# A delta-net kernel whose 32x32 forward substitutions move from VectorE to GpSimd

## The chip, the cores and the metric

The kernel runs on one core of one Trainium2 chip. The metric is the device time of one execution in microseconds, lower is better. Each core has TensorE (PE, matmuls, with weight loads shown apart as PEld), VectorE (DVE), ScalarE (ACT), GpSimd (POOL) and SyncE (SP, which here only issues DMAs). Every engine works through its own instruction list in order.

## The reference

Three blocks of a small model over 256 positions of width 1024: a gated delta net with a gated MLP, sliding-window attention with a gated MLP, and a block with gated linear attention, latent attention and an MLP. The change touches the first stage only, the delta net:

```python
qkv = silu(causal_dwconv(qkv, conv_w))                  # width 4
m = where(strict, einsum('bnhcd,bnhsd->bnhcs', k_beta, k) * decay, 0.0)
t_mat = triangular_solve(m + eye, eye, left_side=True, lower=True, unit_diagonal=True)
u = einsum('bnhcs,bnhse->bnhce', t_mat, v_beta)
w = einsum('bnhcs,bnhsd->bnhcd', t_mat, k_beta * exp(gc)[..., None])
```

There are 16 heads; for each, and for each stretch of the sequence, a unit lower triangular matrix has to be inverted before the values can be mixed.

## The kernel before

All weights come from HBM as 512 KB tiles of 128x1024 (`wr`, loaded by SP, line 172). Each is split into two matmul operands: ScalarE rounds it (`wh`, line 186) and VectorE takes the difference (`wl`, line 187, two inputs in SBUF). Every product is then three matmuls (lines 249 to 251). Each of `wr`, `wh` and `wl` has four buffers, and one weight tile feeds 8 blocks of 128x128, so 24 matmuls.

The delta-net stage (`gdn_body`) is written as generators. The projections (`gemm`, `gemm_nat`) run one after another in the order of `ORDER`; each fourth weight block calls `tick`, which advances every side generator by one step. The side generators are:

- `conv`, called when a bank of q, k or v is ready: one ScalarE scaling (line 647), six VectorE multiply-adds that read the bank from PSUM (`cy`, line 650), one ScalarE SiLU (line 651).
- `x_stage` makes the triangular matrices in `XA` and writes their diagonal 32x32 blocks to HBM (`s1`, line 714).
- `inv_stage` reads the 128 blocks back, one per partition (`NT`, line 749, a DMA of the GpSimd queue), sets `TI` to the identity (lines 750 and 751, GpSimd) and does the forward substitution in 31 steps of two instructions (lines 757 and 759): step j multiplies a column of `NT` by row j of `TI` into `fst`, (31-j)(j+1) elements a partition, and adds `fst` onto the rows below. Then VectorE transposes each block into `TP` (line 764), SP writes `TI` and `TP` to HBM (lines 765 and 766) and reads them back into `XA` and `T64` in 14 small DMAs (lines 770 and 773).
- `a_stage` makes the attention blocks (`kq`, lines 729 to 733) and `chain`, four times, uses the inverses: `y1p` (line 823), `z1p`, `y2p`, `z2p`, and on to the gated output, whose matmuls with `w_out` end the stage.

The order of the instructions in each engine's list is not that of the code: a planner sorts them when the kernel is built, by the order in the code, but takes a later instruction first when it expects the earlier one not to be ready. `NT`, `TI` and `TP` share two buffers, `fst` has one.

Of the kernel before, what the change touches and what calls it, by code (L numbers as in the profile page):

```python
# [14 lines left out]
ALU = mybir.AluOpType  # L15
# [4 lines left out]
P = 128  # L20
# [122 lines left out]
class Builder:  # L143
# [432 lines left out]
    def gdn_body(self, gp, x):  # L576
        nc, tc, sp = self.nc, self.tc, self.sp
# [166 lines left out]
        def inv_stage():  # L744
            while st["X"] < 8:
                yield
            NT = t4([P, 32, 32], "NT")
            TI = t4([P, 32, 32], "TI")
            Q[1].dma_start(NT, s1.rearrange("b c h s t -> (b c h) s t"))
            nc.gpsimd.memset(TI, 0.0)  # L750
            nc.gpsimd.memset(TI.rearrange("p a b -> p (a b)")[:, 0:1024:33], 1.0)
            for _ in range(INVW):
                yield
            for j in range(31):
                m = 31 - j
                tmp = gp.tile([P, 256], F32, tag="fst", bufs=1, name="fst")[:, : m * (j + 1)].rearrange("p (a b) -> p a b", a=m)
                nc.vector.tensor_tensor(tmp, NT[:, j, j + 1 :].unsqueeze(2).to_broadcast([P, m, j + 1]),  # L757
                                        TI[:, j, 0 : j + 1].unsqueeze(1).to_broadcast([P, m, j + 1]), ALU.mult)
                nc.vector.tensor_tensor(TI[:, j + 1 :, 0 : j + 1], TI[:, j + 1 :, 0 : j + 1], tmp, ALU.add)  # L759
                st["step"] = j + 1  # L760
                if INVS(j):
                    yield
            TP = t4([P, 32, 32], "TP")
            nc.vector.tensor_copy(TP.rearrange("p c i -> p i c"), TI)
            Q[2].dma_start(s3.rearrange("b c h s t -> (b c h) s t"), TP)
            Q[2].dma_start(s2.rearrange("b c h s t -> (b c h) s t"), TI)
            nc.gpsimd.memset(T64[0:32, :, :, 32:64], 0.0)
            for b in range(4):
                for tt in range(2):
                    Q[3].dma_start(XA[blk(b), :, 2 * tt, blk(b)], s3[b, tt].rearrange("h c i -> c h i"))  # L770
                    if b < 3:
                        c = (0, 32, 0)[b]
                        Q[3].dma_start(T64[blk(b), tt, :, c : c + 32], s2[b, tt].rearrange("h i c -> i h c"))
            for _ in range(WINV):
                yield
            st["inv"] = True
# [158 lines left out]
        gz = self.gemm_nat("w_in", x, KD, [4096, 4608, 5120, 5632], 512, evac_z)  # L935
        self.side(x_stage())
        self.side(inv_stage())
        self.side(a_stage())
        for q4 in range(4):
# [995 lines left out]
```

## Time and profile before

| | us |
|---|---|
| median of 3 runs | 1226.88 (1225.82 to 1230.05) |
| the profiled execution | 1229.75 |
| its span | 1228.0 |
| busy PE / DVE / ACT / POOL | 1192.3 / 894.4 / 689.5 / 25.1 |
| the inversion's 62 VectorE instructions, busy | 20.8 |
| first one starts / last one starts | 100.83 / 149.25 |

The profile times every instruction of one execution from the start of its span. Busy is time in which an engine worked; idle time before an instruction is shown in brackets with what ended it. The profiled execution took 1.75 us more than its span.

### The profile page before, as it was taken

What the parts mean: (1) busy time and instruction counts of PE and PEld (TensorE: products, weight loads), DVE (VectorE), ACT (ScalarE), POOL (GpSimd) and SP (SyncE); (2) the same over time, 40 slices, a digit from 0 to 9 for tenths busy, and PEclk for the clock granted to TensorE, in tenths of its full rate; (3) what the DMA queues carried; (4) which work ended last, traced back from release to release, by engine and by line L of the source; (5) the groups of instructions that cost most, each with busy time, mean ns of one, the idle gap of its engine ahead of it and who ended that gap; (6) DMA issues with size and microseconds to landing.
All of it is one profiled execution on the core that took longest, in us unless ns stands there. A gap on an engine that the chain in (4) does not pass through costs nothing.

```text
span 1228.0 us, 23416 instructions
## 1 busy us (share of the span) xinstructions
PE 1192.3 (97%) x9368; PEld 1128.1 (92%) x9368; DVE 894.4 (73%) x1677; ACT 689.5 (56%) x1174; POOL 25.1 (2%) x47
## 2 busy tenths in 40 slices
PE   7999989999699999989999999999999999999997
PEld 6989878999699999979999999989889998999996
DVE  6978966668487778887987777766665567655555
ACT  5786546456265557564755556745465545444443
POOL 2000000000000000000000000000000000000000
PEclk9999999999899999999999999999999999999999
DMA  6546474355975566543465555364245564556562
GB/s 227 169 136 222 141 192 164 111 165 152 166 236 188 189 188 203 175 139 130 162 207 189 185 181 172 101 211 145 91 148 178 188 213 150 174 187 188 180 185 83
DMA packets 68989, 209.13 MB, mean 170 GB/s; under 512 B 18197, under 2 KB 18325, under 8 KB 68624
## 3 DMA queue, kind: packets, MB, share of 16 engines
q1 hardware_dynamic: 65600, 194.77, 49.4%
q0 software_dynamic: 3280, 12.87, 4.5%
q8 instruction: 73, 1.20, 0.4%
q14 instruction: 36, 0.29, 0.1%
HBM read 199.75 MB, written 7.86 MB: 169 GB/s over the span
## 4 chain that ended last, share of the span: by engine, by line
PE 83%; DVE 7%; issue 5%; DMA 3%; ACT 2%; POOL 0%; SPq 0%; DVEq 0%; ACTq 0%; POOLq 0%
PE pb L249 19%; PE pb L251 19%; PE pb L250 19%; PE acc L249 6%; PE acc L250 6%; PE acc L251 6%; DMA wr<-wall 2%; DVE wl L187 2%; DVE cy L650 1%; DMA wzog<-wzd 1%; PE ssb L669 1%; DVE fst L757 0%; DVE TI L759 0%; PE s L1082 0%; PE kv L1541 0%
## 5 line engine op out<-in xcount | busy, mean ns | idle before, releaser
L187 DVE TENSOR_TENSOR wl<-wr,wh 128x1024 fp32r<-128x1024 f32 x362 | 441.2, 1223 | 188.7 <-ACT wh L186 188.1
L186 ACT ACTIVATE wh<-wr 128x1024 fp32r<-128x1024 f32 x362 | 381.4, 1057 | 345.4 <-issue 88.5
L251 PE MATMUL pb<-xh,wl 128*128 128x256 f32 x1224 | 347.7, 284 | 11.4 <-DVE wl L187 11.3
L249 PE MATMUL pb<-xh,wh 128*128 128x256 f32 x1224 | 351.0, 287 | 2.9 <-ACT wh L186 2.4
L250 PE MATMUL pb<-xl,wh 128*128 128x256 f32 x1224 | 346.6, 283 | 0.2 <-DVE xl L570 0.2
L251 PEld LDWEIGHTS pb<-xh,wl 128*128 128x128 f32 x1224 | 232.7, 190 | 12.8 <-DVE wl L187 12.8
L249 PEld LDWEIGHTS pb<-xh,wh 128*128 128x128 f32 x1224 | 233.0, 190 | 5.6 <-ACT wh L186 2.9
L250 PEld LDWEIGHTS pb<-xl,wh 128*128 128x128 f32 x1224 | 233.0, 190 | 0.5 <-DVE xl L570 0.4
L249 PE MATMUL pb<-fh,wh 128*128 128x256 f32 x416 | 118.8, 286 | 0.0
L251 PE MATMUL pb<-fh,wl 128*128 128x256 f32 x416 | 117.6, 283 | 0.0
L250 PE MATMUL pb<-fl,wh 128*128 128x256 f32 x416 | 117.2, 282 | 0.1
L249 PE MATMUL acc<-ah,wh 128*128 128x256 f32 x352 | 98.7, 280 | 0.0
L251 PE MATMUL acc<-ah,wl 128*128 128x256 f32 x352 | 98.6, 280 | 0.0
L250 PE MATMUL acc<-al,wh 128*128 128x256 f32 x352 | 98.6, 280 | 0.0
L250 PEld LDWEIGHTS pb<-fl,wh 128*128 128x128 f32 x416 | 78.8, 189 | 1.2 <-DVE fl L436 0.5
L249 PEld LDWEIGHTS pb<-fh,wh 128*128 128x128 f32 x416 | 78.4, 189 | 1.5 <-issue 0.4
L251 PEld LDWEIGHTS pb<-fh,wl 128*128 128x128 f32 x416 | 78.3, 188 | 0.0
L977 DVE SCALAR_TENSOR_TENSOR fy<-fpad,cols,fy 128x256 f32<-128x256 f32 x176 | 73.6, 479 | 0.0
L249 PE MATMUL pb<-wh,xh 128*128 128x512 f32 (+1 forms) x176 | 70.1, 400 | 0.0
L250 PE MATMUL pb<-wl,xh 128*128 128x512 f32 (+1 forms) x176 | 67.8, 385 | 0.5 <-DVE wl L187 0.5
L251 PE MATMUL pb<-wh,xl 128*128 128x512 f32 (+1 forms) x176 | 67.9, 386 | 0.0
L249 PEld LDWEIGHTS acc<-ah,wh 128*128 128x128 f32 x352 | 66.3, 188 | 0.0
(438 smaller groups left out, 2100.7 us busy)
## 6 DMA issues: line engine op xcount, KB each, us to landing
wr<-wall SPq DMA_DIRECT2D x362, 512.0 KB, 3.7
bd<-brow POOLq DMA_DIRECT2D x1, 3072.0 KB, 36.1
wzd<-zt POOLq DMA_DIRECT2D x8, 256.0 KB, 3.4
wzog<-wzd POOLq DMA_DIRECT2D x4, 512.0 KB, 5.7
bias<-bd POOLq DMA_DIRECT2D x4, 512.0 KB, 6.9
h<-xT SPq DMA_DIRECT2D x4, 256.0 KB, 3.7
h<-xT POOLq DMA_DIRECT2D x1, 1024.0 KB, 5.6
wrow<-wrow POOLq DMA_DIRECT2D x1, 1024.0 KB, 8.7
```

The costliest lines, as they stand in the source:

```text
L186: nc.scalar.activation(hi, r, AF.Copy)
L187: i = nc.vector.tensor_tensor(lo, r, hi.bitcast(F32), ALU.subtract)
L249: mm(out, ah, bh, start=start, stop=False, skip_group_check=skip)
L250: mm(out, ah, bl, start=False, stop=False, skip_group_check=skip)
L251: mm(out, al, bh, start=False, stop=stop, skip_group_check=skip)
L650: nc.vector.scalar_tensor_tensor(y[:, i, n:], u[:, : T - n], w(j), y[:, i, n:], ALU.mult, ALU.add)
L669: nc.tensor.matmul(ssb[:, c : c + 1], sq[:, i, tt * P : tt * P + P], self.ones[:, 0:1], start=True, stop=True)
L977: nc.vector.scalar_tensor_tensor(y[:, i], u[:, i, j : j + T], w(j), y[:, i], ALU.mult, ALU.add)
```

## The change

Both instructions of each of the 31 substitution steps are issued to GpSimd in place of VectorE. Shapes, operands, buffers and their order in the code stay as they are.

```diff
             for j in range(31):
                 m = 31 - j
                 tmp = gp.tile([P, 256], F32, tag="fst", bufs=1, name="fst")[:, : m * (j + 1)].rearrange("p (a b) -> p a b", a=m)
-                nc.vector.tensor_tensor(tmp, NT[:, j, j + 1 :].unsqueeze(2).to_broadcast([P, m, j + 1]),
+                nc.gpsimd.tensor_tensor(tmp, NT[:, j, j + 1 :].unsqueeze(2).to_broadcast([P, m, j + 1]),
                                         TI[:, j, 0 : j + 1].unsqueeze(1).to_broadcast([P, m, j + 1]), ALU.mult)
-                nc.vector.tensor_tensor(TI[:, j + 1 :, 0 : j + 1], TI[:, j + 1 :, 0 : j + 1], tmp, ALU.add)
+                nc.gpsimd.tensor_tensor(TI[:, j + 1 :, 0 : j + 1], TI[:, j + 1 :, 0 : j + 1], tmp, ALU.add)
```

## Rows read from the trace of the kernel before

**Rows 1.** Page, part 1: busy time, share of the span, instructions.

```profile
PE 1192.3 (97%) x9368; PEld 1128.1 (92%) x9368; DVE 894.4 (73%) x1677; ACT 689.5 (56%) x1174; POOL 25.1 (2%) x47
```

**Rows 2.** Windows: stretch, length, busy by engine, granted clock, DMA share, GB/s.

```profile
100.00:150.00 50.00, 48.49 (x365) 46.24 (x366) 48.01 (x129) 27.15 (x41) 1.08 (x2) 1.00 0.50 161
...
110.00:120.00 10.00, 10.00 (x87) 10.00 (x86) 10.00 (x26) 5.10 (x8) 0.00 (x0) 1.00 0.53 171
130.00:140.00 10.00, 8.49 (x70) 8.14 (x69) 9.77 (x33) 5.25 (x9) 0.00 (x0) 1.00 0.10 34
150.00:160.00 10.00, 8.32 (x41) 6.34 (x40) 9.45 (x17) 5.18 (x10) 0.00 (x0) 1.00 1.03 224
170.00:180.00 10.00, 8.27 (x103) 7.53 (x92) 7.50 (x14) 6.63 (x10) 0.00 (x0) 0.90 0.24 69
```

**Rows 3.** Groups of VectorE instructions from 100 to 150 us.

```profile
L187 DVE TENSOR_TENSOR wl<-wr,wh 128x1024 fp32r<-128x1024 f32 x13 | 15.8, 1218 | 1.2 <-ACT wh L186 1.2
L650 DVE SCALAR_TENSOR_TENSOR cy<-pb,cols,cy 128x255 f32<-128x255 f32 (+2 forms) x30 | 14.3, 475 | 0.2 <-ACT cy L647 0.2
L759 DVE TENSOR_TENSOR TI<-TI,fst 128x31 f32<-128x31 f32 (+15 forms) x31 | 10.4, 336 | 0.2
L757 DVE TENSOR_TENSOR fst<-NT,TI 128x31 f32<-128x31 f32 (+15 forms) x31 | 10.4, 334 | 0.1
```

**Rows 4.** Timeline of PE: the matmuls that waited, and the first `y1p`.

```profile
138.34 0.39 PE L251 MATMUL pb<-xh,wl 128*128 128x256 f32 x1 [1.51 <-DVE wl L187]
...
152.85 0.50 PE L250 MATMUL pb<-wl,xh 128*128 128x512 f32 x1 [0.55 <-DVE wl L187]
...
159.36 0.66 PE L789 MATMUL vtp<-ident,vt 128*128 128x128 f32 x4 [1.13 <-ACT vt L651]
...
163.10 0.24 PE L823 MATMUL y1p<-h,XA 32*32 32x32 f32 x2
...
176.77 0.39 PE L251 MATMUL pb<-xh,wl 128*128 128x256 f32 x1 [1.74 <-DVE wl L187]
```

**Rows 5.** Timeline of ScalarE: one weight rounding.

```profile
125.58 1.06 ACT L186 ACTIVATE wh<-wr 128x1024 fp32r<-128x1024 f32 x1 [1.42 <-PE pb L250]
```

**Rows 6.** Timeline of VectorE: first and last substitution, two late subtractions.

```profile
100.83 0.18 DVE L757 TENSOR_TENSOR fst<-NT,TI 128x31 f32<-128x31 f32 x1
...
137.07 1.21 DVE L187 TENSOR_TENSOR wl<-wr,wh 128x1024 fp32r<-128x1024 f32 x1
...
149.25 0.18 DVE L759 TENSOR_TENSOR TI<-TI,fst 128x31 f32<-128x31 f32 x1
...
151.59 1.21 DVE L187 TENSOR_TENSOR wl<-wr,wh 128x1024 fp32r<-128x1024 f32 x1
```

**Rows 7.** Timeline of SP: the inverse written, the next weight loads.

```profile
149.50 0.33 SPq L766 DMA_DIRECT2D s<-TI  x1
...
152.86 0.33 SPq L172 DMA_DIRECT2D wr<-wall  x1
...
161.89 72.54 SPq L172 DMA_DIRECT2D wr<-wall  x16
```

**Rows 8.** The tile `NT`: its one DMA, issue to landing.

```profile
DMA to landing us min/median/max: 5.9/5.9/5.9
```

**Rows 9.** Groups of GpSimd instructions, shapes apart: busy us, mean ns.

```profile
L750 POOL MEMSET TI<- 128x1024 f32 x1 | 1.0, 973 | 0.0
...
L594 POOL MEMSET gch<- 128x384 f32 x1 | 0.4, 422 | 0.0
...
L589 POOL CAST identb<-ident 128x128 bf16<-128x128 f32 x1 | 0.3, 299 | 5.0 <-DMA ident<-cst 5.0
L524 POOL MEMSET ones<- 128x128 f32 x1 | 0.2, 204 | 0.3 <-POOLq L1923 0.3
L751 POOL MEMSET TI<- 128x32 f32 x1 | 0.2, 162 | 0.1
...
L1923 POOL MEMSET const-float32-1.0<- 128x1 f32 x1 | 0.1, 93 | 0.0
```

**Rows 10.** Timeline of VectorE, 14 to 32 us.

```profile
20.99 4.63 DVE L187 TENSOR_TENSOR wl<-wr,wh 128x1024 fp32r<-128x1024 f32 x4
```

**Rows 11.** Timeline of GpSimd, 0 to 100 us.

```profile
20.18 0.95 POOL L767 MEMSET h<- 32x1024 f32 x1 [2.09 <-DVE xn L568]
21.08 4.90 POOL L588 CAST mask3b<-mask 128x384 bf16<-128x384 f32 x1
...
94.79 0.54 POOL L749 DMA_DIRECT2D NT<-s  x1 [17.87 <-DMA s<-XA]
```

## The prediction

> **What bounds the kernel now.** I read the page first, then the windows of the delta-net stage, then who waits inside them. TensorE is busy 1192.3 of 1228.0 us [rows 1], so what a change can win is TensorE's idle time in the stage it touches, and what it can lose is new idle time there. The substitutions run from 100.83 to 149.43 us [rows 6], 48.6 us for 62 instructions that are busy only 20.8 us [rows 3], because VectorE's list alternates them with other work: VectorE is busy 48.0 of the 50 us from 100 to 150 [rows 2]. It is the saturated helper of that stretch, TensorE the engine that sets the end.
>
> TensorE still works without a gap for most of it. Its matmuls come every 10/87 = 0.115 us [rows 2], so one weight tile (24 matmuls) lasts 2.76 us. Four gaps stand between 130 and 180 us [rows 4]: 1.51 us at 138.34 and 0.55 us at 152.85, both ended by a weight subtraction `wl`; 1.13 us at 159.36, ended by a conv's SiLU; 1.74 us at 176.77, again `wl`. The first three are VectorE's backlog. The ninth rounding after 100 us is done by ScalarE at 126.64 [rows 5], its subtraction, the ninth too, starts at 137.07 [rows 6], over 10 us late; the gap at 138.34 follows directly. The subtraction at 151.59 [rows 6] ends the second gap, and it also frees a `wr` buffer: SP issues the next weight load at 152.86 [rows 7], and the ScalarE work in front of the SiLU waits for weights. The fourth gap is less clear: the weight loads also stand behind the inverse's small DMAs, from 152.86 to 161.89 [rows 7], and that remains.
>
> **What the change takes from VectorE.** 62 instructions, 10.4 + 10.4 = 20.8 us [rows 3]. VectorE's load from 100 to 150 us falls from 48.0 to 27.2 us. The subtractions then follow their roundings, and three gaps should close: 1.51 + 0.55 + 1.13 = 3.2 us. I leave the fourth, 1.74 us, for the range. VectorE's saved 20.8 us are worth no more than that, since TensorE has nothing else to wait for.
>
> **What it puts on GpSimd.** The trace before shows no two-input instruction there, so the price is built from the nearest ones [rows 9]. A memset goes from 204 ns for 128 elements to 422 ns for 384: 0.85 ns an element that is written. The smallest takes 93 ns, so about 0.09 us is fixed. The cast of 128 elements, one read and one write, takes 299 ns: (299 - 93)/128 = 1.61 ns, hence 0.76 ns for a read. Two reads and a write: 2.37 ns. The steps have 5456 elements a partition (the sum of (31-j)(j+1) over j = 0 to 30), twice over, 10912: 25.9 us. Fixed: 62 x 0.09 = 5.6 us. Rows of `TI` are not contiguous: the memset of 32 scattered elements takes 162 ns, (162 - 93)/32 = 2.2 ns each against 0.85, so 1.3 ns for a jump; 496 row starts in each of three operands add 1.9 us. Sum 33.4 us undisturbed. Lower bound: an element at the price of the cast, 5.6 + 10912 x 0.00161 = 23.2 us. Upper bound: every element at the scattered ratio 2.2/0.85, that is 6.1 ns, 72 us. I take the middle value, since each of its parts is a row.
>
> GpSimd does not run undisturbed. The cast of 384 elements should take 0.09 + 384 x 0.00161 = 0.7 us; it took 4.90 us, from 21.08 to 25.98 [rows 11], over four subtractions back to back that took 4.63 us from 20.99 to 25.62 [rows 10], the usual 1.16 us each. So GpSimd stood still while VectorE read two SBUF operands, and VectorE lost nothing. From 100 to 150 there are 13 such subtractions [rows 3], 13 x 1.16 = 15.1 us, 30% of the time. The convolutions read their bank from PSUM and one operand from SBUF; I take them as no hindrance. The substitutions then need 33.4/0.70 = 47.9 us, and 1.1 us more for the two GpSimd DMA issues that lie in the window [rows 2]: 49.0 us. They cannot start earlier, since `NT` is issued at 94.79 [rows 11] and takes 5.9 us to land [rows 8], 100.7. They end at 149.8, against 149.4 before: a loss of 0.4 us.
>
> The Trainium skill speaks against the change and for the hindrance. "SBUF — State Buffer", section "Who interferes with whom", says that a VectorE instruction with two SBUF inputs and a GpSimd instruction that reads SBUF use one shared read interface, and that the later one waits for the whole of the earlier. By that rule, the cast's row agrees for GpSimd's side (4.90 us for an estimated 0.7); that a subtraction is held by GpSimd no row here shows. "GPSIMD Engine Reference", section "3. Performance versus the Vector engine", has 4497 ns for a two-input add of 2048 elements; as an estimate from that page 2.2 ns an element, and the sum would be 31.5 us in place of 33.4, the end 146.9 in place of 149.8.
>
> **What waits for the end of the substitutions.** VectorE's transpose copy, SP's write of `TI` and the 14 small DMAs behind it, then `y1p` on TensorE, 163.10 - 149.43 = 13.7 us after the last step [rows 4, 6]. TensorE did not idle before the first `y1p`, so there is little slack: I count each microsecond of delay as one of TensorE time. Behind the copy on VectorE stand the subtractions and convolutions, behind the write on SP the weight loads, behind `y1p` on TensorE the projections. Where the planner puts them matters: it does pull instructions ahead, as the memset of line 767, which the code has behind the substitutions, ran at 20.18 [rows 11]. I assume that it places the copy about where the data are.
>
> GpSimd has no other work to delay but DMA issues (1.1 us in this window [rows 2]); they are queued behind at most one step of 0.7 us. That costs nothing while a spare `zt` buffer covers it, and 0.7 us otherwise.
>
> **Sum.** -3.2 + 0.4 = -2.8 us. The profiled execution, 1229.75 us, becomes 1226.95; it stood 2.87 us above the median of the runs, so the runs become 1226.88 - 2.8 = 1224.1 us. A measurement of this kernel tells about 0.3%, 3.7 us, from no change, so this is a gain near the limit.
>
> **Rivals.**
>
> GpSimd is slower than the rows say, the substitutions end late and TensorE waits at `y1p`: slower. The point from which it decides is close. The gain is eaten when they take 48.6 + 3.2 = 51.8 us; the run is slower by over 3.7 us from 55.5 us, an element price of ((55.5 - 1.1) x 0.70 - 7.5)/10912 = 2.8 ns in place of 2.37. At half as much again, 3.6 ns, it is 46.8/0.70 + 1.1 = 68 us, 19.4 us late, 1226.9 + 19.4 - 3.2 = 1243. For it: the scattered memset's 2.2 ns, and that no row shows two reads; against it: the middle price is put together from undisturbed rows. Chance 0.25.
>
> The planner believes in a faster GpSimd than there is and puts the transpose copy early into VectorE's list. Had it counted the undisturbed 33.4 us, the copy would stand at 134, when GpSimd has 0.30 x 33.4 = 10 us left; VectorE then waits 10 us with the subtractions behind the copy. TensorE has up to three weight tiles in hand, 8.3 us, and fewer if the lead is two, 5.5 us. It idles 1.7 to 4.5 us, and catching up can cost as much again: 1225.5 to 1232, middle 1229. For it: the 20.18 memset shows that it pulls ahead; against it: before, no list was held at the copy. Chance 0.12.
>
> The change does nothing in the end: the subtractions wait for GpSimd as often as GpSimd for them, 13 times up to 0.7 us, or the gaps come from the late weight loads and stay: 1226.9. For it: SP's 9 us of small DMAs [rows 7]. Chance 0.08.
>
> More is won: the fourth gap closes too, and with it the granted clock of 0.90 from 170 to 180 [rows 2], a mean between its levels of 2.4 and 1.2 GHz, is whole again, about 1 us: 1226.9 - 3.2 - 1.7 - 1.0 = 1221. For it: a VectorE at 54% lets weight tiles be prepared deeper, which would bridge SP's 9 us. Chance 0.10.
>
> **How the numbers follow.** The forecast has 0.45, with its own range 1221 to 1227 (GpSimd's end 3 us earlier or later, the fourth gap in or out). About half of it, 0.22, is faster by over 0.3%, 0.23 within. Add 0.10 faster; 0.25 slower; of the planner's case 0.07 slower and 0.05 within; 0.08 within. Faster 0.32, same 0.36, slower 0.32. The range reaches down to 1219 and up to 1239, so that the worst half of the slow GpSimd and a little below are left out.
>
> **What would show it.** Right: VectorE busy about 27 of the 50 us from 100 to 150; subtractions within 2 us of their roundings; the gaps at 138 and 153 us gone; the largest GpSimd steps at 0.7 us alone and near 1.8 us when a subtraction falls on them; the last step near 150 us, `y1p` near 163 without idle time. Wrong: a step of over 0.8 us with no subtraction beside it; an idle VectorE in front of the copy of line 764 or TensorE in front of line 823; convolutions that hold GpSimd as well, which would take 30 x 0.4 us more.

## The result, and the profile after

The changed kernel takes 1250.34 us (median of 4 runs, 1249.14 to 1251.74), the kernel before beside it 1228.36 (1225.82 to 1230.05): ratio 1.0177 [1.0159, 1.0196], about 22 us slower, where 2.8 us less were forecast. The profiled execution took 1249.57 us, its span is 1247.7.

The page of the kernel after, part 1 (busy time) and two rows of part 2 (tenths in 40 slices of 31 us):

```profile
PE 1193.0 (96%) x9368; PEld 1129.3 (91%) x9368; DVE 883.4 (71%) x1615; ACT 689.3 (55%) x1174; POOL 63.6 (5%) x109
...
PE   7999399999889999998999999999999999999997
...
PEclk9999699999989999999999999999999999999999
```

TensorE does the same work in the same busy time [rows 1]. The fifth slice, 125 to 156 us, is at 3 tenths with TensorE's granted clock at 6 tenths: the loss has one place. Windows of the kernel after around it (columns as in [rows 2]), and the whole stage:

```profile
120.00:130.00 10.00, 10.00 (x85) 9.95 (x84) 6.02 (x9) 5.24 (x8) 9.14 (x12) 1.00 0.51 160
130.00:140.00 10.00, 3.98 (x34) 3.78 (x32) 0.00 (x0) 0.00 (x0) 8.88 (x15) 0.85 0.00 0
140.00:150.00 10.00, 0.00 (x0) 0.00 (x0) 1.02 (x2) 0.00 (x0) 7.56 (x18) 0.50 0.00 0
150.00:160.00 10.00, 5.84 (x36) 5.79 (x37) 9.75 (x20) 6.45 (x12) 0.00 (x0) 0.63 0.87 238
...
100.00:260.00 160.00, 136.00 (x1309) 126.87 (x1309) 95.37 (x215) 77.76 (x161) 44.39 (x73) 0.91 0.47 147
```

The same stretch of the kernel before:

```profile
100.00:260.00 160.00, 154.24 (x1476) 144.07 (x1477) 121.13 (x314) 86.51 (x184) 5.92 (x11) 0.99 0.51 160
```

From 130 to 149 us VectorE, ScalarE and the DMA engines stand still, from 134 us TensorE too, and GpSimd alone works. TensorE's idle time in the stage grew from 160 - 154.24 = 5.8 to 160 - 136.00 = 24.0 us, 18.2 of the 19.7 us by which the span grew. What held them is in the waits of PE and of DVE (95 to 300 us: total, times, longest):

```profile
PE vtp L789 <- ACT vt L651: 20.2, 1, 20.2
PE z2p L855 <- ACT Y L848: 2.2, 1, 2.2
PE pb L249 <- ACT wh L186: 1.6, 1, 1.6
```

```profile
DVE TP L764 <- POOL TI L759: 22.8, 1, 22.8
```

One wait of VectorE, at the transpose copy, and one of TensorE. VectorE's timeline:

```profile
124.26 1.57 DVE L187 TENSOR_TENSOR wl<-wr,wh 128x1024 fp32r<-128x1024 f32 x1
125.75 0.47 DVE L650 SCALAR_TENSOR_TENSOR cy<-pb,cols,cy 128x255 f32<-128x255 f32 x1
148.98 1.03 DVE L764 COPY TP<-TI 128x1024 f32<-128x1024 f32 x1 [22.76 <-POOL TI L759]
149.87 0.96 DVE L650 SCALAR_TENSOR_TENSOR cy<-pb,cols,cy 128x254 f32<-128x254 f32 x2
```

The copy stands in VectorE's list between the first and the second multiply-add of a convolution. VectorE reached it at 126.2 us, its data came at 148.95, and the rest of the convolution and all later subtractions waited behind it. ScalarE waited for the convolution: the next `wh` stands in its list behind the convolution's second scaling `cy` (a convolution has two scalings, each with three of the six multiply-adds, not one). TensorE stopped at 154.16 - 20.17 = 133.99, at the transposes `vtp`, which need this convolution's SiLU. ScalarE's and PE's timelines:

```profile
126.04 1.06 ACT L186 ACTIVATE wh<-wr 128x1024 fp32r<-128x1024 f32 x1 [0.48 <-PE pb L250]
150.87 0.47 ACT L647 ACTIVATE cy<-pb,cols 128x256 f32<-128x256 f32 x1 [23.76 <-DVE cy L650]
```

```profile
154.16 1.12 PE L789 MATMUL vtp<-ident,vt 128*128 128x128 f32 x4 [20.17 <-ACT vt L651]
...
180.96 0.85 PE L823 MATMUL y1p<-h,XA 32*32 32x32 f32 x32
```

SP was held as well: between the loads of `wr` and the next ones stand the two writes of the inverse. The last loads in front of them, before the change and after it:

```profile
93.14 54.65 SPq L172 DMA_DIRECT2D wr<-wall  x17
```

```profile
93.58 32.61 SPq L172 DMA_DIRECT2D wr<-wall  x13
150.04 0.33 SPq L765 DMA_DIRECT2D s<-TP  x1
```

Before, 17 loads stood there, now 13. The same can be counted on VectorE: the subtractions in front of the copy, in the kernel before (copy at 149.61) and after, as windows of line 187 alone (stretch, length, busy, count, clock, DMA share, GB/s):

```profile
0.00:149.30 149.30, 47.12 (x39) 1.00 0.54 174
```

```profile
0.00:126.50 126.50, 43.55 (x35) 1.00 0.59 188
```

So the copy and the writes moved ahead by four weight tiles in two lists that are worked off in order, and GpSimd was not done by then. GpSimd's timeline:

```profile
101.67 0.23 POOL L757 TENSOR_TENSOR fst<-NT,TI 128x31 f32<-128x31 f32 x1 [4.72 <-DMA NT<-s]
105.01 0.59 POOL L803 DMA_DIRECT2D wzd<-zt  x1 [3.11 <-ACT zt L802]
105.62 0.28 POOL L759 TENSOR_TENSOR TI<-TI,fst 128x31 f32<-128x31 f32 x1
...
124.82 1.49 POOL L757 TENSOR_TENSOR fst<-NT,TI 128x247 f32<-128x247 f32 x1
...
130.08 0.62 POOL L757 TENSOR_TENSOR fst<-NT,TI 128x256 f32<-128x256 f32 x1
130.78 0.73 POOL L759 TENSOR_TENSOR TI<-TI,fst 128x256 f32<-128x256 f32 x1
131.59 0.64 POOL L757 TENSOR_TENSOR fst<-NT,TI 128x255 f32<-128x255 f32 x1
...
134.51 0.60 POOL L757 TENSOR_TENSOR fst<-NT,TI 128x247 f32<-128x247 f32 x1
...
148.70 0.25 POOL L759 TENSOR_TENSOR TI<-TI,fst 128x31 f32<-128x31 f32 x1
```

The substitutions ran from 101.67 to 148.95 us, 47.3 us. Three things are in that. Step sizes are symmetric about the sixteenth step, and from its end on VectorE stood still: 148.95 - 131.59 = 17.4 us for the last 15 steps, 1.5 for the sixteenth, so 2 x 17.4 + 1.5 = 36.2 us undisturbed. A store of `zt` that stands between the two instructions of step 1 waited 3.1 us for its data and held the step. And instructions beside a subtraction take 1.3 to 1.5 us, where the same shapes alone take 0.3 to 0.7: the one at 124.82, 1.49 us (alone, at 134.51, 0.60), lies beside the subtraction of 124.26, which is itself stretched from the usual 1.22 us [rows 3] to 1.57.

### The profile page after: what moved, and what is told of

It reads as the page before. It is cut to its first block, busy times and chain, and to the rows that moved or that the text cites. A ratio compares the mean times of both kernels' runs of the same rounds, so it can differ in the third digit from the quotient of the medians.

```text
span 1247.7 us, 23427 instructions
## 1 busy us (share of the span) xinstructions
PE 1193.0 (96%) x9368; PEld 1129.3 (91%) x9368; DVE 883.4 (71%) x1615; ACT 689.3 (55%) x1174; POOL 63.6 (5%) x109
## 4 chain that ended last, share of the span: by engine, by line
PE 87%; DVE 5%; POOL 3%; DMA 2%; ACT 2%; issue 1%; SPq 0%; DVEq 0%; ACTq 0%
PE pb L249 20%; PE pb L251 19%; PE pb L250 19%; PE acc L249 7%; PE acc L250 6%; PE acc L251 6%; DMA wr<-wall 2%; POOL fst L757 2%; POOL TI L759 2%; DVE wl L187 1%; PE ssb L669 0%; DMA ident<-cst 0%; PE z2p L855 0%; ACT wh L186 0%; PE y2p L847 0%
```

## The experiments

The theory at first: the copy stands too early in VectorE's list. With pin_copy and copy_on_pool it became: the copy in VectorE's list and the two writes in SP's stand too early, and either list alone holds TensorE. Rivals: GpSimd is simply too slow (moving the copy then gives nothing); the shared access of VectorE and GpSimd costs the time; the relief of VectorE was never worth anything.

**pin_copy**: the copy is tied behind the newest subtraction, so it can't be pulled ahead; the writes are left where they are.

```diff
-            nc.vector.tensor_copy(TP.rearrange("p c i -> p i c"), TI)
+            cp = nc.vector.tensor_copy(TP.rearrange("p c i -> p i c"), TI)
+            self.behind(cp, self.lastwl)
```

> The changed kernel, with the transpose copy of the inverse (VectorE) tied behind the newest weight subtraction that is traced before it, which puts it four weight subtractions later in VectorE's list, about where it stood before the change. SyncE's write of the inverse still stands in front of the weight load that it also preceded in the changed kernel. Theory (VectorE's list is held 22.8 us at the copy, and TensorE's 20.2 us wait is that): the wait at the copy falls to a few us and the time to 1225 to 1234; what is left over the kernel before comes from SyncE's list. Rival A (SyncE's list, held at the same data, keeps the weights away): 1244 to 1250, with ScalarE's rounding waiting for weight loads. Rival B (the inverse simply comes too late from GpSimd): 1245 to 1250, with TensorE waiting at its first use of the inverse.

1250.24 us against 1229.93, ratio 1.0157 [1.0136, 1.0178]: as slow as the change, so the theory in its first form fell. VectorE's wait fell from 22.8 to 12.6 us, but ScalarE's timeline names another releaser:

```profile
158.34 1.06 ACT L186 ACTIVATE wh<-wr 128x1024 fp32r<-128x1024 f32 x1 [19.03 <-DMA wr<-wall]
```

**copy_on_pool**: the copy runs on GpSimd, behind the last step, so VectorE's list has nothing to wait for; SP's list is unchanged.

```diff
-            nc.vector.tensor_copy(TP.rearrange("p c i -> p i c"), TI)
+            nc.gpsimd.tensor_copy(TP.rearrange("p c i -> p i c"), TI)
```

> The changed kernel, with the transpose copy on GpSimd as well, so that it stands in VectorE's list no more; SyncE's list is that of the changed kernel but for one place. Theory: no wait on VectorE; time 1226 to 1236, the copy costing GpSimd 2 to 3 us more than VectorE's 1.0, which the inverse comes later. Rival A (SyncE's list holds): 1244 to 1250. Rival B (late inverse): 1247 to 1253, a little over the changed kernel.

1249.83 us, 1.0150 [1.0127, 1.0174]. VectorE does not wait at the copy at all, and the time is the same. The waits of ScalarE and the timeline of SP:

```profile
ACT wh L186 <- DMA wr<-wall: 22.8, 2, 21.6
```

```profile
95.50 32.55 SPq L172 DMA_DIRECT2D wr<-wall  x13
157.07 0.33 SPq L765 DMA_DIRECT2D s<-TP  x1
```

No weight load is issued for 29 us. The time lies in the ranges of both rivals, but a late inverse would stop TensorE where it first uses it; its one long wait, 18.6 us, is at `vtp` again, whose SiLU stands in ScalarE's list behind a rounding that waits for weights. SP's list alone costs as much as the change.

**pin_writes** is the counterpart: only the two writes are tied, behind the newest weight load, and the copy stays early.

```diff
-            Q[2].dma_start(s3.rearrange("b c h s t -> (b c h) s t"), TP)
-            Q[2].dma_start(s2.rearrange("b c h s t -> (b c h) s t"), TI)
+            self.behind(Q[2].dma_start(s3.rearrange("b c h s t -> (b c h) s t"), TP), self.lastwr)
+            self.behind(Q[2].dma_start(s2.rearrange("b c h s t -> (b c h) s t"), TI), self.lastwr)
```

> The changed kernel with only SyncE's two writes tied back by two weight loads; the copy stands early in VectorE's list, as in the changed kernel. Theory: VectorE is held as before, 1247 to 1252. Rival A: the weights come, 1225 to 1235. Rival B: 1245 to 1250.

1254.32 us, 2 us over its forecast, 1.0188 [1.0167, 1.0209]; SP issued 15 loads ahead of the writes and reached them at 156.5 us, after the inverse was there, but VectorE's wait is 22.8 us again and TensorE's 20.2. VectorE's list alone costs as much, too: two holds side by side, and neither removal alone gives anything.

**pin_copy_and_writes**: both edits together.

> As the kernel with the copy tied back, and SyncE's two writes of the inverse tied behind the newest weight load traced before them, so that two more weight loads stand in front of them. Theory: neither list is held long; the backlog of VectorE is gone; 1222 to 1228, which is the prediction's sum. Rival A predicts the same here, and a drop of 15 us or more from the kernel with the copy alone tied back. Rival B: still 1245 to 1250.

1247.84 us, 1.0136 [1.0109, 1.0163], a miss. Its waits:

```profile
DVE TP L765 <- POOL TI L760: 12.6, 1, 12.6
```

```profile
PE vtp L791 <- ACT vt L652: 11.4, 1, 11.4
```

The tie holds the copy only behind the subtraction that is newest when the code reaches it. 39 subtractions stand ahead of it again, as before the change, but VectorE, freed of the steps, is there at 142.5 us, while the inverse is ready at 155.0. So the code itself has to reach the copy later.

TensorE's long wait fell by 8.8 us, the span of the profiled execution by 1.1 only (1247.7 to 1246.6). The rest shows in the page:

```profile
PE 1198.5 (96%) x9368; PEld 1133.9 (91%) x9368; DVE 883.9 (71%) x1615; ACT 689.2 (55%) x1174; POOL 63.5 (5%) x109
```

From 100 to 260 us TensorE idles 17.8 us, 6.2 less than in the changed kernel, but the same matmuls keep it busy 5.5 us longer. From 180 to 185 us, at a granted clock of 0.53, most of them last 0.41 us each, where the same shape lasts 0.28 at 1.00.

**both_late**: eight more turns of the side generator ahead of the copy, both ties, and `WINV`, the turns between the read-back and `chain`, cut from 10 to 4 to give six of them back.

```diff
-WINV = 10
+WINV = 4
...
+            for _ in range(8):
+                yield
             TP = t4([P, 32, 32], "TP")
```

> The changed kernel with the copy and both writes traced eight ticks later and tied behind the newest weight subtraction and the newest weight load of that moment (on VectorE six weight tiles later than in the changed kernel, on SyncE seven weight loads later); the ticks from the loads of the inverse to its first use are cut from 10 to 4, so that TensorE's list has its first use about where it stood before. Theory now (any one of the lists, VectorE's at the copy or SyncE's at the writes, that reaches the inverse before GpSimd has it stops TensorE; the inverse is ready at about 155 us if VectorE keeps running): no list waits over 3 us for the inverse except TensorE's at its first use; 1224 to 1233. Rival B (the inverse comes too late in itself, 155 in place of 149 us): TensorE waits 6 us or more at the first use and the time is 1233 to 1242. Rival C (GpSimd's port use slows VectorE's subtractions so that weights stay late): TensorE waits at subtractions all through 100 to 155 us, 1235 or more.

1232.96 us against 1229.04, 1.0034 [1.0014, 1.0054]. 43 subtractions now stand ahead of the copy and 18 of the 22 us are gone, though the inverse is ready later than in the changed kernel (157.2 us for 149.0) and GpSimd's instructions fall on subtractions as before. So the places in the lists are shown to be the cause of all but 4 us. Windows, VectorE's copy, and TensorE's two longest waits (95 to 300 us):

```profile
130.00:140.00 10.00, 10.00 (x86) 9.95 (x85) 9.14 (x19) 6.16 (x10) 9.14 (x12) 1.00 0.49 154
...
150.00:160.00 10.00, 10.00 (x59) 8.70 (x58) 6.47 (x14) 5.64 (x8) 7.47 (x16) 1.00 0.27 84
160.00:170.00 10.00, 9.02 (x75) 8.74 (x74) 4.34 (x9) 1.06 (x1) 0.00 (x0) 1.00 0.79 210
170.00:180.00 10.00, 6.40 (x109) 5.40 (x108) 5.83 (x14) 4.17 (x9) 0.00 (x0) 0.76 0.80 244
```

```profile
157.20 1.13 DVE L767 COPY TP<-TI 128x1024 f32<-128x1024 f32 x1 [3.53 <-POOL TI L760]
```

```profile
PE y2p L851 <- ACT h L839: 3.7, 2, 1.9
PE y1p L827 <- DMA h<-s: 2.2, 3, 1.0
```

TensorE works without a gap from 100 to 160 us: the three gaps of [rows 4] are closed, as predicted. The inverse is ready at 157.16, not 149.4, and the loss is now in the late chains behind it: all 8.0 us of TensorE's idle time there (160 - 151.96) are waits inside them. **both_late_use_later** is the same with `WINV` left at 10.

> The same, with the first use of the inverse left 10 ticks behind its loads, so later in TensorE's list. Theory: 1224 to 1235; if TensorE's wait at the first use is what is left in the sister kernel, it is gone here, and the end of the delta-net stage pays for the later chains. Rival B: 1233 to 1245. Rival C: 1235 or more.

1234.80 us, 1.0055 [1.0035, 1.0076]: using the inverse still later wins nothing, and what both_late won does not hang on `WINV`.

**no_substitution** leaves out the 62 instructions (`TI` stays the identity), so its time is the relief of VectorE with an inverse that costs nothing.

> The kernel without the 62 substitution instructions (the identity is used in place of the inverses), everything else as it was. It shows what VectorE's relief and an early inverse are worth together at most. The prediction's gap reading: 1220 to 1225. If the gaps come from SyncE's small DMAs and not from VectorE: 1226 to 1229.

1225.51 us, between the two forecasts, 0.9966 [0.9948, 0.9984]: by the ratio 4.2 us of 1229.04 (2.0 to 6.4). TensorE's busy time in the stage, against 154.24 before, and its only wait from 95 to 300 us:

```profile
100.00:260.00 160.00, 157.68 (x1510) 148.88 (x1510) 111.25 (x254) 88.48 (x187) 5.93 (x11) 0.98 0.53 167
```

```profile
PE z2p L859 <- ACT Y L852: 2.2, 1, 2.2
```

157.68 - 154.24 = 3.4 us less idle time: all four gaps of [rows 4] are closed, and a wait of 2.2 us in a chain is new. With these lists moving the substitutions can hardly win more than this.

**late_z_on_act**: both_late, and ScalarE issues the stores of `zt`, so that GpSimd's list holds nothing but the steps.

```diff
-            nc.gpsimd.dma_start(wzd[(c - 4096) // 512, :, tt], zt)
+            nc.scalar.dma_start(wzd[(c - 4096) // 512, :, tt], zt)
```

> The kernel with copy and writes placed late, and the stores of the z projection issued by ScalarE instead of GpSimd: in GpSimd's list two of them stood behind the first substitution instruction and the first waited 3 us for its data. Theory: the inverse is ready 3 to 4 us earlier, near 153 us; the first use of it on TensorE waits less; 1229 to 1232. If the late inverse is not what is left: no change, 1233.

1230.18 us against 1229.81, 1.0003 [0.9988, 1.0017]: level with the kernel before, the best with substitutions on GpSimd. The steps ran from 102.83 to 154.74, 51.9 us, 16 of their 62 instructions over 1.1 us long. **before_z_on_act** makes the same edit alone to the kernel before.

> Control: the kernel before, substitutions on VectorE, with the z stores issued by ScalarE in place of GpSimd. If the 2.5 us that late_z_on_act ended its inverse earlier came from freeing GpSimd's list alone, this edit does nothing here, where GpSimd has nothing behind the stores: ratio within 0.997 to 1.003, the substitutions from about 101 to 149.5 us and the gaps near 138 and 153 us as before. Rival: the stores are better placed on ScalarE whatever runs on GpSimd, and this kernel is 1 to 4 us faster than before; then late_z_on_act owes its tie to the store and not to GpSimd's list.

1230.42 against 1230.65, 0.9999 [0.9979, 1.0019]: nothing by itself (its substitutions ran from 102.7 to 151.5 us, 2 us later than forecast). The interval of both_late, [1.0014, 1.0054], just overlaps that of late_z_on_act, so that the store is worth the 3 us is likely, not certain.

**vector_late_lists**: both_late with the substitutions on VectorE again, the control for the lists.

> The kernel before (substitutions on VectorE) with copy and writes placed late, as a control: the same places in the lists and four ticks to the first use, without GpSimd. Theory (what is left over the kernel before in the late kernel is the inverse, ready on GpSimd at 157 us against 149): here the copy is reached at about 152 to 155 us, 1228 to 1232, 1 to 4 us under the late kernel on GpSimd. If the places in the lists alone cost it: 1233. If they are a gain by themselves: under 1227.

1236.36 us, 1.0051 [1.0031, 1.0071], 4 us more than forecast. VectorE's backlog is back, in PE's timeline as the old gap:

```profile
140.62 0.39 PE L252 MATMUL pb<-xh,wl 128*128 128x256 f32 x1 [1.48 <-DVE wl L187]
```

The last step is done at 151.7, but VectorE gets to the copy only at 161.20. Beside late_z_on_act, on the same chip, this is 6 us slower: with equal places in the lists, 43 subtractions ahead of the copy in both, GpSimd is the better engine for the steps (the stores of `zt`, which differ too, are worth nothing here by before_z_on_act).

**mid_z_on_act**: late_z_on_act with five turns in place of eight and `WINV` 7.

> As the late kernel with the z stores on ScalarE, but with the copy and writes five ticks later in place of eight, and seven ticks in place of four to the first use. Theory: with the inverse near 153 us the lists reach it about 3 us too early, so 1 to 3 us of VectorE's wait at the copy, under the weight tiles in hand: 1228 to 1232; if a list is held over 8 us: 1235 or more.

1239.17 us, 1.0079 [1.0053, 1.0106], a miss. VectorE's timeline and PE's:

```profile
148.14 0.47 DVE L651 SCALAR_TENSOR_TENSOR cy<-pb,cols,cy 128x254 f32<-128x254 f32 x1
151.76 1.10 DVE L767 COPY TP<-TI 128x1024 f32<-128x1024 f32 x1 [3.15 <-POOL TI L760]
152.70 0.46 DVE L651 SCALAR_TENSOR_TENSOR cy<-pb,cols,cy 128x253 f32<-128x253 f32 x1
```

```profile
156.89 0.97 PE L793 MATMUL vtp<-ident,vt 128*128 128x128 f32 x4 [4.13 <-ACT vt L652]
```

A wait of 3.15 us costs TensorE 4.13 us, while 3.53 us in both_late cost it nothing there. Here the copy stands inside a convolution, for which TensorE's next transpose waits; there a subtraction, with a weight tile in hand, was next. The wait is not the whole 9 us: from 100 to 260 us TensorE idles 11.4 us in place of 6.0 in late_z_on_act, and over the whole execution it is busy 3.6 us longer (1194.9 for 1191.3 us), in the stage at a granted clock of 0.96 in place of 0.98.

## Why the prediction was wrong

**The step that failed** is "I assume that it places the copy about where the data are". The lists show 35 subtractions ahead of the copy in place of 39, and 13 loads ahead of the writes in place of 17; GpSimd's data came 22.8 us after VectorE got there. Nor would the old place have done: in pin_copy_and_writes, with 39 ahead again, VectorE was there 7.1 us earlier than before the change (142.5 for 149.6) and the inverse came 5.6 us later (155.0 for 149.4), which together are its wait of 12.6 us. The copy had to move back in the list (behind 43 it did, in both_late), and it moved ahead. That the planner counts a step on GpSimd for less than it takes is an inference from this placement: no run shows its prices.

**The rival was named and priced too low.** The early copy was given 10 us of VectorE's wait, 1229 us in all, and a chance of 0.12. It put VectorE's arrival at 134 and the end of the steps at 144; they were 126.2 and 148.95, so 22.8 us. The cover was right in size: TensorE lasted from 126.2 to 134.0, 7.8 us (forecast 5.5 to 8.3), though what stopped it were the transposes that need the held convolution, not the end of its weight tiles. The restart was not counted: from the copy at 149.0 to the transpose at 154.2, 5.2 us. 22.8 - 7.8 + 5.2 = 20.2, TensorE's wait. And the weight loads behind the writes on SP, which the prediction names, got no price, though copy_on_pool shows that they hold TensorE nearly as long, 18.6 us, by themselves.

**GpSimd's end was nearly right by luck.** The end came at 148.95, forecast 149.8. The undisturbed sum is 36.2 us, not 33.4: the fixed part was too low, the price of an element too high. From the rows, (0.62 - 0.24)/225 = 1.7 ns an element for the multiply and, by 0.73 and 0.25, 2.1 ns for the add, in place of 2.37; and the smallest instruction, 0.24 us less 0.05 for its 31 elements, with the 0.08 us until the next one (130.08 + 0.62 to 130.78), leaves 0.27 us fixed, in place of the 0.09 from [rows 9]. These two errors nearly cancel. The hindrance of 30% held: 36.2/0.70 = 51.7, and late_z_on_act took 51.9, with 16 hits of about 1 us in place of 13 of 1.16. The forecast end came true only because VectorE stood still for half of it; with VectorE running and the store in the way it is 157.2 (both_late), 55.6 us, the very length from which the first rival called the run measurably slower: 1.0034.

**VectorE's load did not fall to 27.2 of 50 us.** In both_late, where nothing holds it, it is busy for 43.4 from 100 to 150 us: it does 17 subtractions there in place of 13 and 34 multiply-adds in place of 30 [rows 3]. And 20.8 us was too much to subtract: neighbours overlap on VectorE, so that the four groups of [rows 3] alone add up to 50.9 us in a window in which it was busy for 48.0 [rows 2].

**"VectorE lost nothing" was wrong.** Ten subtractions from 100 to 126 us average 1.35 us against 1.22 [rows 3]. The Trainium skill, "SBUF — State Buffer", section "Who interferes with whom", says that the ports which VectorE and GpSimd share are an exclusive lock, and that the order of issue decides which of the two waits. The rows agree, either way round: an instruction of 0.6 us took 1.49 and a subtraction 1.57. In late_z_on_act it cost GpSimd (51.9 - 36.2)/16 = 1 us for each of the 16 long ones; it cost VectorE a tenth of its subtractions' time, and TensorE nothing that shows from 100 to 160 us in both_late.

**The DMA issues cost more than 1.1 us.** The first waited 3.1 us for its data, with step 1's second half behind it; I had only thought of the issues waiting behind the steps.

**The relief was right.** 3.2 us were forecast for three gaps; no_substitution closes them and the fourth, which the prediction left for the range, and idles 3.4 us less in all. That is about the most that the change could win, and an inverse that is ready 5.3 us (late_z_on_act) to 7.7 us (both_late) after the 149.43 of [rows 6] uses it up: with steps that take 51.9 us the balance is zero, and the first rival had put that point at 51.8.

## What to carry to other kernels

When work moves to a slower engine, look first at every engine that waits for its end and works in a list fixed at build time: the consumer's place in the list is part of the change, and so are the writes on the DMA-issuing engine. The old place need not do, since an engine that has been relieved gets there sooner. Price each such list by itself, since one that is left early costs as much as all of them, and look at what stands directly behind the waiting instruction. Bound the gain by leaving the work out altogether: here 3.4 us, less than any of the risks.

## What the runs showed of the hardware

By the estimate above a GpSimd instruction with two inputs costs 0.27 us besides its elements, so 62 of them 17 of the 36.2 us. From 140 to 150 us, without a matmul, TensorE's granted clock read 0.50, the 1.2 GHz level, and from 150 to 160, where it started again, 0.63, a mean between that level and 2.4 GHz. It was not foreseen that a store to HBM that waits for its data holds the GpSimd instructions behind it: 3.1 us here.
